# Forty of block 0's weighted rows on the tensor engine in a decoder layer

## The chip, the cores and the metric

The kernel runs on one core of one Trainium2 chip. Time is device time in microseconds, from the first to the last instruction of the program. The program's instructions are put in order once, before it runs: a scheduler lays out a queue for each engine (PE for matrix products, DVE for vectors, ACT for scalar functions and copies, POOL, which here issues the gathers, and SP, which issues the other loads and stores), and each engine works through its queue in that order, waiting on semaphores.

## The reference

One decoder layer over 512 tokens of width 1024, all in float32. The input projection feeds two groups of heads, and their outputs go through one output projection, a residual and a layer norm. Then comes a feed-forward part in which each token picks 128 of 16,384 single-neuron experts:

```python
proj = x @ w_in
att_out = dsa_attention(q_att, rms_norm(c_kv), q_idx, k_idx, w_idx, w_uk, w_uv)  # 128 best causal keys a query
hg_out = hgrn2(hg_q, hg_f, hg_i, hg_gate, lower_bound, g_norm)                   # gated recurrence, chunks of 32
mix = concatenate([att_out, hg_out]) @ w_out
h = layer_norm(ALPHA * x + mix)
# feed-forward, per token t: 8 heads x 16 experts
s = einsum('thpd,hpkd->thpk', h @ w_q, sub_keys)      # two sets of 128 scores a head
experts, g = top 16 of the sums of the two top-16 sets, softmax over them
a = gelu(einsum('td,thkd->thk', h, u[experts]))
ffn = einsum('thk,thkd->td', g * a, v[experts])
y = layer_norm(ALPHA * h + ffn)
```

## The kernel before

The 512 tokens are four blocks of 128. A first stage takes block 0 through attention, recurrence, output projection, layer norm and the choice of its experts. A second stage does that for blocks 1, 2 and 3 together. Last comes the dense part: for blocks 2 and 3 all 16,384 experts are computed as matrix products, with the weights of the chosen ones and zeros elsewhere.

Blocks 0 and 1 get their experts as rows instead. For rank k a gather (L639, an indirect DMA that POOL issues) brings the k-th expert's row of u, or later of v, of all 128 tokens into a tile of 128x1024, 512 KB. A row of u is multiplied with the block's `hs` and summed on DVE (L663), which gives one column of `hd`; through gelu and the routing weights these columns become `gate`. A row of v is added to `hs`, weighted with its column of `gate` (L676, DVE). Of block 0's 128 rows of v the last 52 go to PE: ACT makes a diagonal matrix `dg` out of a column of `gate` (L692), two products of 128x512 add the row into two PSUM banks (L694, four passes of PE in the trace), and one DVE add for each bank brings the sum to `hs` (L699). 14 of them stand at the end of stage 2 (`pv`), 38 at the start of the dense part (`pw`); block 1's 256 rows run beside the dense part.

Block 0's rows are spread over stage 2 by hand: `pump(n)` takes the next n rows from the generator `peer_gather`, and the table PUMP says how many at each place (`"hgrn"` 1 at each of eight places and two at another, `"att"` 4 in each half of an attention block, `"mix"` 1, `"q0"` 7). Rows on DVE are pinned to the program's order; everything else the scheduler places where its own timing puts it.

A gather needs a free tile. There are four of its own (GB), and the tiles `hs1`, `hs2`, `hs3`, `hx0`, `hx1` that the kernel doesn't need yet are lent to it (`lent`), nine in turn. `mix_norm` takes `hs1` to `hs3` back for blocks 1 to 3 and loads x into them (L479).

The order of stage 2 in the program: projections, the choice of keys (`select`), the recurrence `hgrn` of blocks 1, 2 and 3, the projection `qa` of the attention's queries, `attention` of the three blocks, `mix_norm`, `queries`. In `attention` PE makes qlp (L429) from `qa`, then the scores `sp` (L439), DVE turns them into P with the row's extreme (L441), ACT takes the exponential, PE transposes (L451) and multiplies (L457, L463), and DVE writes the result into `mixT` (L470). Half a block's four heads are one turn of this. `mix_norm` multiplies `mixT` with the output weights (L491), DVE adds (L494) and does the layer norm (L131 to L144); `queries` transposes the result (hT, L213), projects it (pq, L523), makes scores (L527) and picks the top 16 with MAX8 and its kin (L537 on).

Of the kernel before, what the change touches and what calls it, by code (L numbers as in the profile page):

```python
# [9 lines left out]
F32 = mybir.dt.float32  # L10
# [5 lines left out]
ALU = mybir.AluOpType  # L16
# [9 lines left out]

HGB = 5
GB = 4
UB = 4
VB = 3  # L30
HLB = 6
# [4 lines left out]
PUMP = {"cw": 4, "qi": 4, "hf": 4, "hq": 4, "hi": 4, "hg": 3, "qa": 2, "hgrn": 1, "att": 4, "mix": 1, "sel": 2,  # L36
        "q0": 7, "q1": 0, "q2": 0, "q3": 0}

PEK1 = 14
PEK2 = 38  # L40
PEPRE = 8
# [10 lines left out]
def tile_decoder_layer(ctx, tc, a, out):  # L52
# [218 lines left out]
    def hgrn(b, pr, mixT):  # L271
# [7 lines left out]
        nc.scalar.activation(kk, f, AF.Copy, scale=-1.0, bias=1.0)  # L279
        if b:  # L280
            pump(PUMP["hgrn"])
        cp = bank(f"cum{b}", "hg")
        nc.tensor.matmul(cp, tri, lf, start=True, stop=True)
        rp = bank(f"rev{b}", "hg")
# [6 lines left out]
        nc.vector.tensor_tensor(qs, qs, e, op=ALU.mult)  # L291
        if b:
            pump(PUMP["hgrn"])
        kt = k2(f"kt{b}")
        nc.scalar.activation(kt, cp, AF.Exp, scale=-1.0)
        nc.vector.tensor_tensor(kt, kk, kt, op=ALU.mult)
# [4 lines left out]
        nc.scalar.activation(dec.rearrange("p a b -> p (a b)"), dp[:, :16], AF.Exp)  # L301
        if b:
            pump(PUMP["hgrn"])
        qT = transpose4(qs, f"hqT{b}", nc.scalar, tag="hg")
        kT = transpose4(kt, f"hkT{b}", nc.scalar, tag="hg")
        AT = [k2(f"AT{b}_{par}").rearrange("p (j t) -> p j t", j=4) for par in range(2)]
# [9 lines left out]
        for n in range(4):  # L316
            S.append(state[0])
            if b:
                pump(PUMP["hgrn"])
            dsp = bank(f"ds{b}_{n}", "hg")  # L320
            for h in range(8):
                nc.tensor.matmul(dsp[(h % 2) * 64:(h % 2) * 64 + 64, (h // 2) * 64:(h // 2) * 64 + 64],
                                 kk[n * 32:n * 32 + 32, h * 64:h * 64 + 64],
                                 v[n * 32:n * 32 + 32, h * 64:h * 64 + 64], start=True, stop=True)
            s_new = pre.tile([128, 4, 64], F32, name=f"S{b}_{n}", tag="hg_S", bufs=5)
            ds3 = dsp[:, :256].rearrange("p (j e) -> p j e", j=4)
            nc.vector.tensor_tensor(s_new, state[0], dec[:, :, n:n + 1].to_broadcast([128, 4, 64]), op=ALU.mult)
            nc.vector.tensor_tensor(s_new, s_new, ds3, op=ALU.add)
            state[0] = s_new
        if b:  # L330
            pump(PUMP["hgrn"])
        ot = k2(f"o{b}")
        o = ot.rearrange("p (j a e) -> p j a e", j=4, a=2)
        gs4 = gs.rearrange("p (j a e) -> p j a e", j=4, a=2)
# [322 lines left out]
    def peer_gather(b):  # L657

        hd = cst.tile([128, 128], F32, name=f"hd{b}", tag="hd")
        for k in range(128):  # L660
            g = gather(a["u"], b, k, "u")
            tc.keep_in_program_order(
                nc.vector.scalar_tensor_tensor(g, g, 1.0, hs[b], op0=ALU.mult, op1=ALU.mult,  # L663
                                               accum_out=hd[:, k:k + 1]))
            if k % 32 == 31:
                sl = slice(k - 31, k + 1)
                nc.scalar.activation(hd[:, sl], hd[:, sl], AF.Gelu_apprx_tanh)
                nc.vector.tensor_tensor(gate[:, b, sl], gate[:, b, sl], hd[:, sl], op=ALU.mult)
            rows[0] -= 1
            yield True  # L670
        weighted.add(b)
        tc.keep_in_program_order(nc.scalar.mul(hs[b], hs[b], ALPHA))
        for k in range(128 - (PEK1 + PEK2 if b == 0 else 0)):
            g = gather(a["v"], b, k, "v")
            tc.keep_in_program_order(
                nc.vector.scalar_tensor_tensor(hs[b], g, gate[:, b, k:k + 1], hs[b], op0=ALU.mult, op1=ALU.add))  # L676
            rows[0] -= 1
            yield True
        spent.add(b)

    weighted = set()
    spent = set()

    def pe_gather(n, p):

        while 0 not in weighted:
            pump(1)
        ks = [pe_left.pop(0) for _ in range(n)]
        for k in ks:
            g = gather(a["v"], 0, k, "v")  # L690
            dg = gat.tile([128, 128], F32, name=f"dg{k}", tag="dg", bufs=1)
            nc.scalar.mul(dg, ident, gate[:, 0, k:k + 1])  # L692
            for i in range(2):
                nc.tensor.matmul(p[i], dg, g[:, i * 512:(i + 1) * 512], start=(k == ks[0]), stop=(k == ks[-1]))  # L694
            if k != ks[-1]:
                yield
        for i in range(2):
            y = hs[0][:, i * 512:(i + 1) * 512]
            nc.vector.tensor_tensor(y, y, p[i], op=ALU.add)  # L699
        yield  # L700

    todo = []
    rows = [512 - PEK1 - PEK2]

    def pump(n):
        while n > 0 and todo:
            try:
                if not next(todo[0]):
                    return
                n -= 1  # L710
            except StopIteration:
                todo.pop(0)

    def dense(den, dps):
# [88 lines left out]
                    nc.tensor.matmul(acc[i][n], wt[:, sl], vt, start=(j == 0 and q == 0), stop=(j == 127 and q == 2))  # L803

        def residual():
            ia = gat.tile([128, 128], F32, name="ia", tag="dg", bufs=1)
            nc.scalar.mul(ia, ident, ALPHA)
            for i in range(nb):
                for n in range(2):
# [34 lines left out]
    def stage(blocks, xT):  # L844
# [12 lines left out]
        else:  # L857
# [3 lines left out]
            kv_norm(blocks, pr)  # L861
            pens = {b: select(b, pr[b]) for b in blocks}
            hp = hgrn_proj(blocks, xT)
        for i, b in enumerate(blocks):
            hgrn(b, hp[b], mixT[:, 4:8, i * 128:(i + 1) * 128])
        if blocks != [0]:
            feat_proj(blocks, xT, pr, "qa")
        for i, b in enumerate(blocks):
            attention(b, pr[b], pens[b], mixT[:, 0:4, i * 128:(i + 1) * 128])
        mix_norm(blocks, mixT)  # L870
# [72 lines left out]
```

## Time and profile before

| | us |
|---|---|
| median of 3 runs | 1611.0 (1610.07 to 1612.66) |
| the profiled execution | 1606.46 |
| its span | 1604.6 |
| DVE busy in it | 1383.7 |
| PE busy in it | 1446.5 |
| rows of v on DVE, blocks 0 and 1 (L676) | 261.4 |
| rows of u on DVE, blocks 0 and 1 (L663) | 307.2 |

L676 counts 204 instructions, 76 of block 0 and 128 of block 1; L663 and each of the two gather lines count 256. The profile names a waiting time by what ended it: "<-DVE gu L663" is an engine that stood until DVE had finished a row of u, "<-issue" is time in which an engine waited for nothing that the profile shows. A mean granted clock of 1.00 for PE is the 2.4 GHz level, 0.50 the 1.2 GHz level. Where a name stands without its number, as P or gv, the profile has left it out.

### The profile page before, as it was taken

The page shows a single profiled execution, that of the slowest core. Times are in us where ns is not written, and L with a number is a line of the kernel's source. Part 1 is how long each engine was busy: PE and PEld are TensorE (multiplying, and loading weights), DVE is VectorE, ACT ScalarE, POOL GpSimd, SP SyncE. Part 2 cuts the span into 40 slices and gives each one's busy share as a digit, 9 for nine tenths or more (in the row PEclk, how much of TensorE's full clock was granted, in tenths as well). Part 3 has the DMA queues.
Part 4 walks back from the last instruction along what each step waited for, and adds up shares of the span by engine and source line. Part 5 has one row for each costly group of instructions (what it writes and reads, how often), then busy time and mean ns, then how long its engine had stood idle before and what let it go on. Part 6 is the DMA issues. An engine that isn't in the chain of part 4 may idle for free. (4 is left out here: it accounts for less than half of the span.)

```text
span 1604.6 us, 24491 instructions
## 1 busy us (share of the span) xinstructions
PE 1446.5 (90%) x7858; PEld 1087.4 (68%) x7858; DVE 1383.7 (86%) x3263; ACT 708.0 (44%) x1501; POOL 673.9 (42%) x531
## 2 busy tenths in 40 slices
PE   8889899854788899789989999999999999999996
PEld 4568444543444565246668888888898889889995
DVE  4139999799966899998877989999998899999998
ACT  3302331122432122169984555555555555555553
POOL 0004633777744420355433444444443345534440
PEclk9999999855799899899999999999999999999998
DMA  8378987899967770467668999999999999999995
GB/s 291 125 277 301 348 268 232 290 344 330 351 242 255 263 285 11 145 203 222 218 235 301 350 340 337 353 349 352 352 357 326 336 349 362 351 352 350 355 367 189
DMA packets 166161, 467.89 MB, mean 292 GB/s; under 512 B 18576, under 2 KB 18704, under 8 KB 165904
## 3 DMA queue, kind: packets, MB, share of 16 engines
q0 software_dynamic: 73728, 268.47, 48.0%
q1 hardware_dynamic: 92304, 197.86, 34.3%
q8 instruction: 62, 1.02, 0.2%
q14 instruction: 67, 0.55, 0.1%
HBM read 464.16 MB, written 2.10 MB: 291 GB/s over the span
## 5 line engine op out<-in xcount | busy, mean ns | idle before, releaser
L639 POOL DMA_INDIRECT gv<-in_v_dram,idx x256 | 333.1, 1301 | 417.4 <-DVE hs L676 263.3
L639 POOL DMA_INDIRECT gu<-in_u_dram,idx x256 | 330.9, 1293 | 409.8 <-DVE gu L663 259.1
L663 DVE SCALAR_TENSOR_TENSOR gu<-gu,hs 128x1024 f32<-128x1024 f32 x256 | 307.2, 1222 | 28.0 <-DMA gu<-in_u_dram,idx 27.8
L676 DVE SCALAR_TENSOR_TENSOR hs<-gv,gate,hs 128x1024 f32<-128x1024 f32 x204 | 261.4, 1281 | 9.7 <-DMA gv<-in_v_dram,idx 7.8
L772 ACT CAST v_0h<-v 128x512 fp32r<-128x512 f32 x128 | 79.7, 623 | 95.7 <-PE acc L803 60.9
L523 PE MATMUL pq<-hT,wpq 128*128 128x128 f32 (+1 forms) x512 | 121.3, 396 | 0.0
L774 DVE TENSOR_TENSOR u_0l<-u,u_0h 128x512 fp32r<-128x512 f32 x128 | 88.5, 691 | 35.6 <-ACT u_0h L772 32.6
L772 ACT CAST v_1h<-v 128x512 fp32r<-128x512 f32 x128 | 79.5, 621 | 87.7 <-DMA v<-in_v_dram 42.8
L772 ACT CAST u_0h<-u 128x512 fp32r<-128x512 f32 x128 | 79.4, 620 | 78.0 <-PE hp L783 41.1
L803 PE MATMUL acc<-v_0h,wl 128*128 128x512 f32 x256 | 102.0, 399 | 4.9 <-DVE wl L793 4.9
L523 PEld LDWEIGHTS pq<-hT,wpq 128*128 128x128 f32 x512 | 81.2, 201 | 33.4 <-issue 3.9
L803 PE MATMUL acc<-v_0h,wh 128*128 128x512 f32 x256 | 101.0, 395 | 0.0
L772 ACT CAST u_1h<-u 128x512 fp32r<-128x512 f32 x128 | 79.4, 621 | 48.2 <-PE acc L803 44.6
L774 DVE TENSOR_TENSOR v_1l<-v,v_1h 128x512 fp32r<-128x512 f32 x128 | 87.8, 686 | 14.3 <-ACT v_1h L772 13.5
L803 PE MATMUL acc<-v_1h,wh 128*128 128x512 f32 x256 | 99.7, 389 | 0.0
L803 PE MATMUL acc<-v_1h,wl 128*128 128x512 f32 x256 | 99.7, 389 | 0.0
L803 PE MATMUL acc<-v_0l,wh 128*128 128x512 f32 x256 | 99.5, 390 | 0.0
L774 DVE TENSOR_TENSOR u_1l<-u,u_1h 128x512 fp32r<-128x512 f32 x128 | 87.7, 685 | 4.5 <-ACT wh L791 3.5
L783 PE MATMUL hp<-hTl,u_0h 128*128 128x256 f32 x512 | 84.3, 287 | 8.0 <-ACT u_0h L772 8.0
L783 PEld LDWEIGHTS hp<-hTl,u_0h 128*128 128x128 f32 x512 | 76.7, 189 | 20.8 <-ACT u_0h L772 12.4
L774 DVE TENSOR_TENSOR v_0l<-v,v_0h 128x512 fp32r<-128x512 f32 x128 | 88.1, 688 | 2.5 <-ACT v_0h L772 1.6
L783 PE MATMUL hp<-hTh,u_1l 128*128 128x256 f32 x512 | 83.9, 286 | 5.1 <-DVE u_1l L774 5.1
(277 smaller groups left out, 3137.9 us busy)
## 6 DMA issues: line engine op xcount, KB each, us to landing
v<-in_v_dram SPq DMA_DIRECT2D x256, 256.0 KB, 6.2
u<-in_ut_dram SPq DMA_DIRECT2D x256, 256.0 KB, 6.0
wpq<-in_w_pq_dram SPq DMA_DIRECT2D x32, 512.0 KB, 4.7
wo<-in_w_o_dram SPq DMA_DIRECT2D x16, 512.0 KB, 7.6
hfw<-in_w_hf_dram SPq DMA_DIRECT2D x8, 512.0 KB, 6.8
hqw<-in_w_hq_dram SPq DMA_DIRECT2D x8, 512.0 KB, 9.1
hiw<-in_w_hi_dram SPq DMA_DIRECT2D x8, 512.0 KB, 4.9
qaw<-in_w_qa_dram SPq DMA_DIRECT2D x8, 512.0 KB, 5.1
```

What stands on the lines that cost most here:

```text
L523: nc.tensor.matmul(qp[:, :nt], w[:, k, :], hT[:, k, :nt], start=(k == 0), stop=(k == 7))
L639: nc.gpsimd.indirect_dma_start(out=t, out_offset=None, in_=table, in_offset=bass.IndirectOffsetOnAxis(ap=idx[b][k // 64][:, k % 64:k % 64 ...
L663: nc.vector.scalar_tensor_tensor(g, g, 1.0, hs[b], op0=ALU.mult, op1=ALU.mult, accum_out=hd[:, k:k + 1]))
L676: nc.vector.scalar_tensor_tensor(hs[b], g, gate[:, b, k:k + 1], hs[b], op0=ALU.mult, op1=ALU.add))
L772: nc.scalar.copy(h, x)
L774: nc.vector.tensor_tensor(l, x, h.bitcast(F32), op=ALU.subtract)
L783: nc.tensor.matmul(hp, ut[:, k * 128:(k + 1) * 128], ht[n][:, k, :], start=(n + q + k == 0), stop=(n == 1 and q == 2 and k == 3))
L803: nc.tensor.matmul(acc[i][n], wt[:, sl], vt, start=(j == 0 and q == 0), stop=(j == 127 and q == 2))
```

## The change

The first 40 rows of v of block 0 (PEK0) go to PE as well, in a new generator `pe_head`. It takes the tile `hx1` out of the lent ones and makes it an accumulator `vacc`, so eight tiles are left for gathers. Each row is gathered, gets its `dg` from ACT and is added by two products into two banks `ph`, the first of the two pinned to the program's order. After each eighth row the banks are brought to `vacc`: the first time by two ACT copies, then four times by two DVE adds of 128x512. At the end one DVE add of 128x1024 brings `vacc` to `hs0`. `pump_pe` asks for one row at each of eight places in hgrn 1 and for two at each in hgrn 2 and 3; what is left is asked for behind hgrn 3, where the order of the program now has no `qa` any more, since its projection is called ahead of hgrn. DVE keeps 36 rows of v of block 0 (40 to 75). There are two buffers for `dg` where there was one. The total that the dense part spreads over its loop (`rows`) takes off the 40.

```diff
+DGB = 2
+PEK0 = 40
@@ hgrn: at eight places
         if b:
             pump(PUMP["hgrn"])
+            pump_pe(min(b, 2))
@@ peer_gather
-        for k in range(128 - (PEK1 + PEK2 if b == 0 else 0)):
+        for k in range(PEK0, 128 - PEK1 - PEK2) if b == 0 else range(128):
@@ new
+    def pe_head():
+        lent.remove("hx1")
+        vacc = cst.tile([128, 1024], F32, name="vacc", tag="hx1")
+        for k in range(PEK0):
+            if k % 8 == 0:
+                p = [bank(f"ph{k}_{i}") for i in range(2)]
+            g = gather(a["v"], 0, k, "v")
+            dg = gat.tile([128, 128], F32, name=f"dg{k}", tag="dg", bufs=DGB)
+            nc.scalar.mul(dg, ident, gate[:, 0, k:k + 1])
+            for i in range(2):
+                mm = nc.tensor.matmul(p[i], dg, g[:, i * 512:(i + 1) * 512], start=(k % 8 == 0), stop=(k % 8 == 7))
+                if i == 0:
+                    tc.keep_in_program_order(mm)
+            if k % 8 == 7:
+                for i in range(2):
+                    y = vacc[:, i * 512:(i + 1) * 512]
+                    if k == 7:
+                        nc.scalar.copy(y, p[i])
+                    else:
+                        nc.vector.tensor_tensor(y, y, p[i], op=ALU.add)
+            yield
+        while 0 not in weighted:
+            pump(1)
+        nc.vector.tensor_tensor(hs[0], hs[0], vacc, op=ALU.add)
+        yield
+    def pump_pe(n):
+        if not head:
+            head.append(pe_head())
+        for _ in range(n):
+            next(head[0], None)
@@ pe_gather (and the same for ia in residual)
-            dg = gat.tile([128, 128], F32, name=f"dg{k}", tag="dg", bufs=1)
+            dg = gat.tile([128, 128], F32, name=f"dg{k}", tag="dg", bufs=DGB)
@@
-    rows = [512 - PEK1 - PEK2]
+    rows = [512 - PEK0 - PEK1 - PEK2]
@@ stage
+        if blocks != [0]:
+            feat_proj(blocks, xT, pr, "qa")
         for i, b in enumerate(blocks):
             hgrn(b, hp[b], mixT[:, 4:8, i * 128:(i + 1) * 128])
         if blocks != [0]:
-            feat_proj(blocks, xT, pr, "qa")
+            pump_pe(PEK0 + 1)
```

On PE, in the kernel before, the first scores of block 1's attention (sp1_0 to sp1_2) stand between the last products of hgrn 1 (o1_1, hoT1) and the first of hgrn 2 (cum2):

```order
L344 MATMUL o1_1_2186<-S1_0_2106,hqT1_2071 32x64
L344 MATMUL o1_1_2186<-S1_1_2121,hqT1_2071 32x64
L344 MATMUL o1_1_2186<-S1_2_2136,hqT1_2071 32x64
L439 MATMUL sp1_0_2752<-ckvT_102,qlT1_2736 128x256
L439 MATMUL sp1_1_2757<-ckvT_102,qlT1_2736 128x256
L439 MATMUL sp1_2_2762<-ckvT_102,qlT1_2736 128x256
L213 MATMUL hoT1_ps_2233<-ident_61,o1_2157 128x128 x4
```

In the changed kernel the scores of block 1 stand among the last of the 40 rows (ph32, the banks of rows 32 to 39):

```order
L699 MATMUL ph32_0_2818<-gv0_37_2880,dg37_2882 128x512
L699 MATMUL ph32_1_2819<-gv0_37_2880,dg37_2882 128x512
L446 MATMUL sp1_0_3014<-ckvT_102,qlT1_2998 128x256
L699 MATMUL ph32_0_2818<-gv0_38_2901,dg38_2903 128x512
L699 MATMUL ph32_1_2819<-gv0_38_2901,dg38_2903 128x512
L699 MATMUL ph32_0_2818<-gv0_39_2907,dg39_2909 128x512
L699 MATMUL ph32_1_2819<-gv0_39_2907,dg39_2909 128x512
L446 MATMUL sp1_1_3019<-ckvT_102,qlT1_2998 128x256
L446 MATMUL sp1_2_3024<-ckvT_102,qlT1_2998 128x256
```

hgrn 2 and 3 and rows 0 to 37 stand ahead of sp1_0 now, and two more rows ahead of sp1_1.

On DVE, in the kernel before, the first P of block 1 stand behind a row of u, gu0_125, and the first multiplication of hgrn 3's output (S3 and o3 are of hgrn 3):

```order
L663 SCALAR_TENSOR_TENSOR gu0_123_2333,hd0_1170<-gu0_123_2333,hs0_104 128x1024
L328 TENSOR_TENSOR S3_3_2572<-S3_3_2572,ds3_3_2563 128x256
L663 SCALAR_TENSOR_TENSOR gu0_124_2348,hd0_1170<-gu0_124_2348,hs0_104 128x1024
L663 SCALAR_TENSOR_TENSOR gu0_125_2363,hd0_1170<-gu0_125_2363,hs0_104 128x1024
L351 TENSOR_TENSOR o3_2578<-o3_0_2581,gs3_2027 128x4x64
L441 ISA P1_0_2754,nmx1_2749<-sp1_0_2752,isc1_1380 128x256
L441 ISA nmx1_2749 128x1
L441 ISA P1_1_2759,nmx1_2749<-sp1_1_2757,isc1_1380 128x256
```

In the changed kernel rows of v and the adds into vacc stand ahead of them:

```order
L683 SCALAR_TENSOR_TENSOR hs0_104<-gv0_53_2844,gate_114,hs0_104 128x1024
L683 SCALAR_TENSOR_TENSOR hs0_104<-gv0_54_2871,gate_114,hs0_104 128x1024
L683 SCALAR_TENSOR_TENSOR hs0_104<-gv0_55_2898,gate_114,hs0_104 128x1024
L448 ISA P1_0_3016,nmx1_3011<-sp1_0_3014,isc1_1380 128x256
L448 ISA nmx1_3011 128x1
L683 SCALAR_TENSOR_TENSOR hs0_104<-gv0_56_2970,gate_114,hs0_104 128x1024
L708 TENSOR_TENSOR vacc_2116<-vacc_2116,ph32_0_2818 128x512
L683 SCALAR_TENSOR_TENSOR hs0_104<-gv0_57_2973,gate_114,hs0_104 128x1024
L708 TENSOR_TENSOR vacc_2116<-vacc_2116,ph32_1_2819 128x512
L448 ISA P1_1_3021,nmx1_3011<-sp1_1_3019,isc1_1380 128x256
```

All rows of u, rows 40 to 55 of v and the adds of ph8 to ph24 stand ahead of P1_0 now, rows 56 and 57 and the adds of ph32 ahead of P1_1. On POOL the first 108 gathers are the same in both kernels; behind them the rows of v of the two engines are interleaved with the last 20 rows of u, gv0_55 is the 182nd gather, gv0_39 the 183rd and gv0_57 the 186th.

## Rows read from the trace of the kernel before

**Rows 1.** Page: busy time by engine; groups: busy and mean ns | idle before.

```profile
PE 1446.5 (90%) x7858; PEld 1087.4 (68%) x7858; DVE 1383.7 (86%) x3263; ACT 708.0 (44%) x1501; POOL 673.9 (42%) x531
...
L676 DVE SCALAR_TENSOR_TENSOR hs<-gv,gate,hs 128x1024 f32<-128x1024 f32 x204 | 261.4, 1281 | 9.7 <-DMA gv<-in_v_dram,idx 7.8
```

**Rows 2.** Busy time by stretches: length, engines (instructions), PE clock, DMA, GB/s.

```profile
284.12:465.02 180.90, 119.50 (x686) 72.98 (x684) 165.82 (x311) 49.99 (x135) 142.65 (x116) 0.69 0.92 333
320.00:340.00 20.00, 10.31 (x42) 6.52 (x39) 19.43 (x46) 8.27 (x19) 14.61 (x12) 0.59 0.99 385
320.00:416.00 96.00, 51.09 (x394) 35.72 (x391) 93.20 (x199) 28.00 (x79) 74.50 (x61) 0.52 0.94 346
365.00:374.00 9.00, 0.00 (x0) 0.00 (x0) 9.00 (x21) 0.00 (x0) 6.87 (x8) 0.50 0.97 352
405.20:434.90 29.70, 20.02 (x86) 10.97 (x86) 28.54 (x55) 14.45 (x38) 23.72 (x21) 0.73 0.97 357
434.90:467.70 32.80, 27.27 (x101) 13.50 (x100) 27.07 (x36) 10.76 (x27) 24.60 (x22) 0.95 0.92 334
437.15:454.54 17.39, 14.74 (x50) 6.90 (x49) 17.07 (x23) 4.88 (x14) 13.73 (x12) 1.00 0.91 326
467.70:502.30 34.60, 29.19 (x105) 13.62 (x103) 18.95 (x32) 13.39 (x29) 6.38 (x6) 1.00 0.45 148
540.00:582.00 42.00, 42.00 (x141) 25.73 (x140) 34.25 (x50) 6.01 (x13) 27.88 (x24) 0.95 0.97 370
640.00:668.00 28.00, 23.02 (x59) 9.22 (x58) 28.00 (x186) 6.06 (x14) 11.25 (x10) 1.00 0.58 169
```

**Rows 3.** DVE timeline: start, length, line, operation [idle before <- releaser].

```profile
405.24 0.41 DVE L441 CUSTOM_DVE_ANT_0 P<-sp,isc 128x256 f32<-128x256 f32 x1
...
405.58 0.41 DVE L441 CUSTOM_DVE_ANT_0 P<-sp,isc 128x256 f32<-128x256 f32 x1
...
501.58 0.69 DVE L470 TENSOR_TENSOR mixT<-oT,rT 128x512 f32<-128x512 f32 x1 [1.33 <-ACT rT L108]
...
575.85 0.48 DVE L537 MAX8 sv<-pss 128x8 f32<-128x128 f32 x2
```

**Rows 4.** POOL timeline, three gathers.

```profile
367.10 0.94 POOL L639 DMA_INDIRECT gu<-in_u_dram,idx  x1 [0.30 <-issue]
...
400.51 1.17 POOL L639 DMA_INDIRECT gv<-in_v_dram,idx  x1 [0.30 <-issue]
...
464.05 0.94 POOL L639 DMA_INDIRECT gv<-in_v_dram,idx  x1 [0.30 <-issue]
```

**Rows 5.** Groups by line, POOL, 284 to 465 us.

```profile
L639 POOL DMA_INDIRECT gu<-in_u_dram,idx x71 | 91.1, 1284 | 28.3 <-issue 16.5 <-DVE gu L663 6.1 <-DVE rs_thg L118 1.5
L639 POOL DMA_INDIRECT gv<-in_v_dram,idx x43 | 50.5, 1175 | 13.3 <-issue 10.5 <-DVE nmx L441 1.8 <-DVE rs_thg L119 0.6
```

**Rows 6.** Groups by line, PE, 640 to 668 us.

```profile
L694 PE MATMUL pv<-gv,dg 128*128 128x512 f32 x43 | 21.2, 614 | 5.0 <-ACT dg L692 5.0
```

**Rows 7.** PE timeline, first row after a wait.

```profile
674.89 3.78 PE L694 MATMUL pv<-gv,dg 128*128 128x512 f32 x4 [6.28 <-ACT dg L692]
```

**Rows 8.** DMA issues, 284 to 465 us: count, median us to landing.

```profile
gu<-in_u_dram,idx POOLq DMA_INDIRECT x71, 6.3
gv<-in_v_dram,idx POOLq DMA_INDIRECT x43, 6.2
```

**Rows 9.** Groups by line, DVE, 405.2 to 502.3 and 502.3 to 575.8 us.

```profile
L676 DVE SCALAR_TENSOR_TENSOR hs<-gv,gate,hs 128x1024 f32<-128x1024 f32 x43 | 55.4, 1288 | 0.8
...
L676 DVE SCALAR_TENSOR_TENSOR hs<-gv,gate,hs 128x1024 f32<-128x1024 f32 x32 | 41.1, 1284 | 7.8 <-DMA gv<-in_v_dram,idx 7.0
```

**Rows 10.** PE timeline, mix and two transposes of hT.

```profile
502.33 27.73 PE L491 MATMUL mix<-wo,mixT 128*128 128x512 f32 x64 [1.46 <-DVE mixT L470]
...
533.67 1.56 PE L213 MATMUL hT_ps<-ident,hs 128*128 128x128 f32 x8 [1.62 <-DVE vel L134]
538.34 1.94 PE L213 MATMUL hT_ps<-ident,hs 128*128 128x128 f32 x8 [3.11 <-DVE hs L144]
```

More of the change, by code (lines that the diff above doesn't have):

```diff
@@ L293, in hgrn @@
             pump(PUMP["hgrn"])
+            pump_pe(min(b, 2))
         kt = k2(f"kt{b}")
@@ L303, in hgrn @@
             pump(PUMP["hgrn"])
+            pump_pe(min(b, 2))
         qT = transpose4(qs, f"hqT{b}", nc.scalar, tag="hg")
@@ L319, in hgrn @@
                 pump(PUMP["hgrn"])
+                pump_pe(min(b, 2))
             dsp = bank(f"ds{b}_{n}", "hg")
@@ L331, in hgrn @@
             pump(PUMP["hgrn"])
+            pump_pe(min(b, 2))
         ot = k2(f"o{b}")
@@ L679, in peer_gather @@
         spent.add(b)
+    def pe_head():
[23 more added lines that the diff above has]
+        yield
+    head = []
+    def pump_pe(n):
[3 more added lines that the diff above has]
+            next(head[0], None)
     weighted = set()
@@ L805, in residual @@
         def residual():
-            ia = gat.tile([128, 128], F32, name="ia", tag="dg", bufs=1)
+            ia = gat.tile([128, 128], F32, name="ia", tag="dg", bufs=DGB)
             nc.scalar.mul(ia, ident, ALPHA)
```

## The prediction

> **What bounds the kernel now.** I read the page first, then the busy time by stretches, then the timelines of DVE and POOL over 367 to 576 us, then the groups by line inside the same stretches. On the page DVE and PE both look full [rows 1], which says nothing yet about the part that changes. By stretches it is clearer [rows 2]: from 284 to 465 us DVE is busy 165.8 of 180.9 us while the DMA engines stand at 0.92 and PE at a mean granted clock of 0.69; from 540 to 582 us PE has no idle time at all (42.00 of 42.00). The 40 rows that leave DVE come out of a stretch where DVE and the gathers are both close to full.
>
> What releases the next piece of the layer is read from the DVE timeline [rows 3]. The first P of block 1 runs at 405.24 us, the second at 405.58, the last mixT (block 3) at 501.58, the first top-k instruction at 575.85. Behind that one come the routing and the dense part, in which the change touches nothing but the number of dg buffers; so the end of the program moves by what the first top-k instruction moves.
>
> Next the gathers, which POOL issues one by one. gv_0 is the 129th, issued at 400.51; the 171st is issued at 464.05, and counted back from gv_0 the one at 367.10 is the 108th, gu_107 [rows 4]. Through here POOL waits for almost nothing that another engine does: before the 114 gathers of 284 to 465 us 27.0 us of its idle time are "issue" (16.5 + 10.5) and 6.1 a wait for a tile that DVE's rows free [rows 5]. So the gathers set their own pace. It is 1.59 us each from 367.10 to 400.51 (21 intervals), 1.51 from 400.51 to 464.05 (42), 1.45 inside 437.15 to 454.54 (12 in 17.39 us [rows 2]), and 1.24 at the quickest, as at 367.10 (0.94 and the 0.30 ahead of it).
>
> **The change part by part.** *Work that leaves DVE.* 40 of L676 at 1.281 us [rows 1] are 51.2 us less. Added on DVE are 8 adds of 128x512 out of PSUM, for which mixT, 128x512 out of PSUM as well, has a row of 0.69 us [rows 3], and one add of 128x1024, about one L676: 5.5 + 1.3 = 6.8 us. Net 44.4 us less. That is the gain, and it counts only where DVE is what the next stage waits for.
>
> *Where the 40 rows now stand.* In the kernel before, the P instructions of block 1 stand in DVE's queue right after gu_125, and their sp in PE's queue ahead of hgrn 2. In the changed one the first P stands behind gv_55 and the second behind gv_57 and the adds of ph32; on PE sp1_1 stands behind the matmuls of gv_39. Each engine runs its queue in order, so block 1's attention can't get going before those gathers have landed. In POOL's queue all gathers up to the 108th are the same in both kernels; gv_55 is the 182nd now, gv_39 the 183rd, gv_57 the 186th, where 126 were needed ahead of the first P.
>
> *Its price.* From 367.10 on, hgrn 3 lies beside the next 21 gathers as before, at 1.59 us, to 400.5; the 54 from there to the 183rd are plain rows, for which I take the 1.45 of the stretch that holds only such rows and attention: 78.3 us, an issue at 478.8. A gather lands 6.3 us after its issue (gu; gv 6.2 [rows 8]); then the row's four passes on PE, of which 43 take 21.2 us at full clock, are 1.98 us [rows 6]. 478.8 + 6.3 + 2.0 = 487.1, so the second P runs at about 487.4 in place of 405.58: **+82 us**. The ends: all 75 gathers from 367.10 on at 1.24 are 93.0 us, P at 468.7 (+63); all at 1.59 are 119.3, P at 495.0 (+89). The diag matrix on ACT costs nothing here: PE waits 5.0 us for 43 passes' worth of it with one buffer [rows 6], and now there are two, beside gathers that come slower than PE's rows.
>
> The Trainium skill, "DMA: Bandwidth & Descriptors", section "Where 436 GB/s comes from", holds that a transfer between HBM and SBUF is bound on HBM's side at about 358 GB/s; the 524,288 bytes of a gather would then need 1.46 us, an estimate, none could run closer than that, and P would come at +80 at least. The trace disagrees, with 385 GB/s over 320 to 340 us [rows 2], so 1.24 stays the lower end.
>
> *What is won back in attention.* From the second P to the last mixT it takes 96.0 us now. DVE runs 43 rows of L676 in it [rows 9]; after the change 18 stand behind the second P, and one add of 128x1024. Blocks 1 and 2, where DVE is busy 28.5 of 29.7 and 27.1 of 32.8 us [rows 2], become looser; block 3, with 18.95 of 34.6, is bound by its own chain already. PE's work over the three is 20.0 + 27.3 + 29.2 = 76.5 us, so less than about 75 is not to be had; the other end is no gain. I take 85, the middle: **-11 us** (0 to -21).
>
> *What is won back in mix and the queries.* 32 rows of L676, 41.1 us of DVE, stand between 502.3 and 575.8 us, with 7.0 us of waiting for gv [rows 9]; after the change none. But the stretch is PE's: mix takes 27.73 us in one piece, two transposes of hT are held up 1.62 and 3.11 us by the layer norm on DVE [rows 10], and then pq runs without a gap. The holds, 4.7 us, are what the rows' absence can give back: **-5 us** (-3 to -8).
>
> *Small edits.* With two dg buffers the rows of pv can lose PE's 5.0 us of waiting for dg, but DVE is full there (28.00 of 28.00 us in 640 to 668 [rows 2]): -1 us (0 to -1.5). The loads of hs for blocks 1 to 3 wait for tiles that the gathers borrow, and those are given back at another time: between nothing and one landing of 6.3 us (512 KB as well): +2 us (0 to +6). qa's projection ahead of hgrn moves PE work into a stretch where PE is half idle (51.1 of 96.0 us busy in 320 to 416 [rows 2]): 0. One tile fewer for gathers (8 for 9): a tile's turn of 0.94 + 6.3 + 1.28 = 8.5 us over 8 tiles allows one gather per 1.07 us, below the 1.24: 0.
>
> **Sum.** +82 - 11 - 5 - 1 + 2 = +67 us on a span of 1604.6 us. The profiled execution took 1606.46 us and the median of the runs is 1611.0, 4.5 us above it; the sum is set on the median: **1678 us**. Ends: 63 - 21 - 8 - 1.5 + 0 = +32 (1643) and 89 - 0 - 3 - 0 + 6 = +92 (1703).
>
> **Rivals.** *The gathers catch up.* PE takes two rows of three, tiles come free sooner, gathers go at 1.24 throughout, and a lean DVE lets attention run at PE's 75 us: +32 to +45, some 1649 us. For it: in 365 to 374 us POOL did issue 8 in 9.00 us, with the DMA engines at 0.97 [rows 2]. Against it: POOL waits for tiles only 6.1 us now, so that free tiles can hardly hasten it.
>
> Another cause of slow gathers would be DVE. The Trainium skill, "SBUF — State Buffer", section "SBUF: two separate sides", says that while DVE runs in a mode that takes both ports, GpSimd can't write the descriptors of its DMAs; if rows of L663 and L676 did that, fewer of them on DVE would free the gathers and this rival would hold. The trace speaks against it: the quick gathers of 365 to 374 us fall where DVE has no idle time at all, 9.00 of 9.00 us [rows 2].
>
> *PE is the new bound.* Where PE comes out of a wait its clock is 0.50 (the 1.2 GHz level) and a row takes 3.78 us [rows 7]; in 320 to 416 us the mean granted clock is 0.52 [rows 2]. If the 34 rows from gv_6 on ran so from about 403 us, they would end at 403 + 34 x 3.78 = 531, P at +126, and with the same gains the time were some 1720 us. Against it: with rows close behind one another the clock stood at 1.00 in 640 to 668 us.
>
> *DVE sets the end after all* (the other side): if the P instructions were not held by the order, 44.4 us less DVE work between 367 and 502 us would make the layer faster, 1611 - 44 = 1567 us. It needs 186 gathers by about 405 us, where the program has made 131 by then, and decides only if the second P comes before about 420 us (what attention and queries win back is 16). Nothing speaks for it but DVE's row on the page.
>
> **How the numbers follow.** Forecast 0.62, gathers catch up 0.19, PE the new bound 0.12, DVE the end 0.04, delay and gains cancel 0.03. The range is the sum's two ends, 1643 to 1703; it leaves out the PE case, the faster one and the one that cancels. A difference below 0.2% (about 3 us) can't be told from none here. Faster 0.04, the same 0.02, slower 0.94.
>
> **What would show it.** In the profile after: the second P of block 1 near 487 us (460 to 470 would mean that the gathers caught up, over 510 a slow PE, under 420 that I misread the queues); gathers from 400 to 479 us at 1.4 to 1.5 us each with POOL waiting for "issue"; DVE with idle time ahead of P that ends with gv or with PE's ph; PE's rows at 1.98 us; from the first top-k instruction on the same picture as now, some 67 us later. What would make it wrong above all: gathers that wait for tiles held by either of two consumers, PE or DVE, which the trace of before can't show.

## The result, and the profile after

| | before | changed |
|---|---|---|
| median of 4 runs, us | 1611.83 (1610.07 to 1617.54) | 1691.76 (1684.93 to 1696.68) |
| ratio | | 1.0478 (95%: 1.0435 to 1.0521) |
| span of the profiled execution, us | 1604.6 | 1686.7 |

The change makes the kernel 80 us slower. The prediction was 1678 us, 1643 to 1703, so it held; the delay is 13 us longer than the sum. By the page of the changed kernel, DVE has lost 42 us of work (1383.7 to 1341.6 [rows 1]) and PE has gained 60:

```profile
PE 1506.2 (89%) x8018; PEld 1114.8 (66%) x8018; DVE 1341.6 (80%) x3232; ACT 724.9 (43%) x1543; POOL 660.4 (39%) x531
...
L683 DVE SCALAR_TENSOR_TENSOR hs<-gv,gate,hs 128x1024 f32<-128x1024 f32 x164 | 209.8, 1279 | 33.9 <-DMA gv<-in_v_dram,idx 32.9
```

Where the time went is read from a few instructions of the DVE timeline, those of [rows 3], here in the changed kernel (the first two P of block 1, mixT of block 3, the first top-k):

```profile
494.12 0.42 DVE L448 CUSTOM_DVE_ANT_0 P<-sp,isc 128x256 f32<-128x256 f32 x1 [2.70 <-PE sp L446]
...
499.09 0.42 DVE L448 CUSTOM_DVE_ANT_0 P<-sp,isc 128x256 f32<-128x256 f32 x1
...
583.36 0.69 DVE L477 TENSOR_TENSOR mixT<-oT,rT 128x512 f32<-128x512 f32 x1 [9.79 <-ACT rT L110]
...
652.52 0.87 DVE L544 MAX8 sv<-pss 128x8 f32<-128x128 f32 x4 [28.23 <-ACT pss L539]
```

| us | before | changed | shift | length of the stretch: change |
|---|---|---|---|---|
| second P of block 1 | 405.6 | 499.1 | +93.5 | +93.5 |
| last mixT | 501.6 | 583.4 | +81.8 | -11.7 |
| first top-k | 575.9 | 652.5 | +76.7 | -5.1 |
| last idx (rows below) | 701.7 | 774.6 | +72.9 | -3.8 |
| first product of the dense loop, acc | 851.1 | 932.6 | +81.5 | +8.6 |
| end of the span | 1604.6 | 1686.7 | +82.1 | +0.6 |

93.5 us are lost ahead of P; attention, mix and queries win back 16.8 and the routing 3.8 (no run here shows why the routing did); between the last idx and the dense loop 8.6 us are lost that the prediction did not have.

The 5.1 us of mix and queries do not come from PE's waiting for the layer norm. By groups of PE from the last mixT to the first top-k, the transposes of hT wait as long as before; here before, then changed:

```profile
L213 PE MATMUL hT_ps<-ident,hs 128*128 128x128 f32 x24 | 4.6, 353 | 5.6 <-DVE hs L144 4.0 <-DVE vel L134 1.6
```

```profile
L215 PE MATMUL hT_ps<-ident,hs 128*128 128x128 f32 x24 | 3.9, 326 | 5.3 <-DVE hs L146 5.3
```

What changed is DVE's queue. Before, ACT's copy of the first scores (pss) starts at 572.5, and the top-k stands behind three rows of v until 575.85; in the changed kernel the copy starts at 651.9 and the top-k, for which DVE sits idle, follows 0.6 us later. That is 2.8 of the 5.1 us; the copy itself comes 2.4 us earlier behind the last mixT.

Ahead of P, the POOL timeline shows the 108th gather, the 129th and the 183rd (gv_39); before, the first two were at 367.10 and 400.51 [rows 4]:

```profile
368.93 1.18 POOL L646 DMA_INDIRECT gu<-in_u_dram,idx  x1 [0.30 <-issue]
...
404.58 0.94 POOL L646 DMA_INDIRECT gv<-in_v_dram,idx  x1 [4.68 <-PE ph L699]
...
485.41 0.93 POOL L646 DMA_INDIRECT gv<-in_v_dram,idx  x1 [0.30 <-issue]
```

The 75 gathers take 116.5 us, 1.55 each. By groups, POOL over these 75 now waits for PE's rows too, 11.9 us, which [rows 5] has not at all:

```profile
L646 POOL DMA_INDIRECT gv<-in_v_dram,idx x54 | 58.1, 1076 | 27.6 <-PE ph L699 11.9 <-issue 11.0 <-DVE hs L683 3.2
L646 POOL DMA_INDIRECT gu<-in_u_dram,idx x21 | 24.4, 1163 | 6.4 <-issue 4.9 <-DVE gu L670 0.3 <-DVE f L276 0.3
```

By stretches (columns as in [rows 2]): 410 to 485.4 us, up to gv_39's issue, and 453.7 to 494 within it, where no hgrn is left; then attention, mix and queries up to the first top-k, the routing, and the dense part's head:

```profile
410.00:485.40 75.40, 63.53 (x199) 27.63 (x199) 30.86 (x46) 18.43 (x55) 53.14 (x51) 0.95 0.96 349
453.70:494.00 40.30, 32.87 (x86) 14.28 (x85) 16.44 (x15) 7.87 (x19) 31.43 (x30) 1.00 1.00 379
...
499.10:583.40 84.30, 72.14 (x274) 35.66 (x274) 40.53 (x76) 32.68 (x77) 22.48 (x20) 0.96 0.40 138
583.40:652.50 69.10, 63.12 (x200) 35.30 (x201) 20.91 (x58) 7.91 (x16) 0.00 (x0) 0.95 0.35 115
652.50:774.60 122.10, 109.92 (x342) 58.97 (x341) 118.15 (x795) 33.20 (x65) 24.26 (x24) 0.96 0.39 127
774.60:932.60 158.00, 126.23 (x684) 91.82 (x683) 125.06 (x239) 136.55 (x329) 57.02 (x53) 0.93 0.61 195
```

From 410 to 485 us DVE is busy 30.9 of 75.4 us: it is not the bound any more. The DMA engines stand at 0.96 and PE is busy for 63.5. In the groups of DVE over 404 to 499 us its rows wait 32.9 us for gv, in those of PE over 404 to 496 the new rows wait 10.1:

```profile
L683 DVE SCALAR_TENSOR_TENSOR hs<-gv,gate,hs 128x1024 f32<-128x1024 f32 x18 | 23.1, 1283 | 33.2 <-DMA gv<-in_v_dram,idx 32.9 <-ACT hs L679 0.3
```

```profile
L699 PE MATMUL ph<-gv,dg 128*128 128x512 f32 x154 | 73.8, 624 | 11.9 <-DMA gv<-in_v_dram,idx 10.1 <-DVE vacc L708 1.8
```

And this is the end of the 40 rows on PE. gv_39, issued at 485.41, ends with the passes of 493.91 to 497.51, 12.1 us after its issue, because PE still has the rows ahead of it to do; sp of the second P comes right behind:

```profile
485.23 3.70 PE L699 MATMUL ph<-gv,dg 128*128 128x512 f32 x8
...
489.94 3.70 PE L699 MATMUL ph<-gv,dg 128*128 128x512 f32 x8
493.48 0.59 PE L446 MATMUL sp<-ckvT,qlT 128*128 128x256 f32 x2
493.91 3.60 PE L699 MATMUL ph<-gv,dg 128*128 128x512 f32 x8
497.35 1.03 PE L446 MATMUL sp<-ckvT,qlT 128*128 128x256 f32 x4
```

### The profile page after: what moved, and what is told of

Its sections match the earlier page's. It is cut to its first block, busy times and chain, and to the rows that moved or that the text cites. A ratio compares the mean times of both kernels' runs of the same rounds, so it can differ in the third digit from the quotient of the medians.

```text
span 1686.7 us, 24843 instructions
## 1 busy us (share of the span) xinstructions
PE 1506.2 (89%) x8018; PEld 1114.8 (66%) x8018; DVE 1341.6 (80%) x3232; ACT 724.9 (43%) x1543; POOL 660.4 (39%) x531
## 5 line engine op out<-in xcount | busy, mean ns | idle before, releaser
L646 POOL DMA_INDIRECT gv<-in_v_dram,idx x256 | 324.9, 1269 | 491.3 <-DVE hs L683 244.9
L646 POOL DMA_INDIRECT gu<-in_u_dram,idx x256 | 325.5, 1271 | 422.8 <-DVE gu L670 243.5
L670 DVE SCALAR_TENSOR_TENSOR gu<-gu,hs 128x1024 f32<-128x1024 f32 x256 | 307.3, 1221 | 15.6 <-DMA gu<-in_u_dram,idx 15.4
L683 DVE SCALAR_TENSOR_TENSOR hs<-gv,gate,hs 128x1024 f32<-128x1024 f32 x164 | 209.8, 1279 | 33.9 <-DMA gv<-in_v_dram,idx 32.9
L736 PE MATMUL pw<-gv,dg 128*128 128x512 f32 x152 | 79.7, 656 | 31.3 <-DMA gv<-in_v_dram,idx 22.9
L789 DVE TENSOR_TENSOR og<-iota,dtr 128x512 f32<-128x512 f32 x128 | 81.4, 686 | 25.7 <-PE gb L798 22.6
```

Of the source, the lines that this page charges most:

```text
L646: nc.gpsimd.indirect_dma_start(out=t, out_offset=None, in_=table, in_offset=bass.IndirectOffsetOnAxis(ap=idx[b][k // 64][:, k % 64:k % 64 ...
L789: nc.vector.tensor_tensor(og[n], iota[:, None, :].to_broadcast([128, 4, 128]), x[n][:, c:c + 4, None].to_broadcast([128, 4, 128]), op=ALU. ...
```

## The experiments

Eleven kernels, in three groups (x1 to x4, x5 to x8, x9 to x11), each on one chip, where the kernel before took 1628.1, 1630.4 and 1617.8 us. So ratios to the kernel before on the same chip are compared (the changed kernel: 1.0478); single instants of these profiles lie up to 4% later than on the first chip (P at 420.0 in x6, where the same 126 rows stand ahead of it as at 405.6 in the kernel before). P stands for the second P of block 1.

**Gathers or PE.** *x1: the 40 rows without their gathers.*

```diff
-            g = gather(a["v"], 0, k, "v")
+            g = consts_loaded["wuv"].rearrange("p a b -> p (a b)")
...
-                mm = nc.tensor.matmul(p[i], dg, g[:, i * 512:(i + 1) * 512], ...)
+                mm = nc.tensor.matmul(p[i], dg, g, ...)
```

> The changed kernel, but the 40 rows on the tensor engine multiply a constant tile that lies in SBUF already: their 40 gathers are left out, everything else of them (diag, two products each, adds) stays. The computation is not the layer's. Theory 'the gathers set when attention begins': gv_57 is now the 146th gather in place of the 186th; 38 gathers after the 108th (368.9) at 1.45 us end at about 424, so the second P of block 1 comes near 435 (499.1 in the changed kernel) and the time falls by some 50 to 60 us, to about 1635. Rival 'the tensor engine is as much the bound': 34 rows behind hgrn 3 at 1.85 us from about 405 to 425 on end at 470 to 488, so the second P comes at 470 to 490 and the time falls by only 5 to 25 us, to 1670 to 1685.

Measured: ratio 1.0291 (1.0225 to 1.0358), 1.9% of 1628 us, 30 us, less than the changed kernel. P, and PE in the stretch ahead of it:

```profile
471.61 0.42 DVE L448 CUSTOM_DVE_ANT_0 P<-sp,isc 128x256 f32<-128x256 f32 x1
```

```profile
403.00:471.00 68.00, 68.00 (x324) 34.11 (x323) 41.83 (x68) 23.93 (x62) 31.37 (x26) 1.00 0.65 215
```

P comes at 471.6, in the rival's range: with no gather of these rows to wait for, PE is busy for 68.00 of 68.00 us at the 2.4 GHz level, and holds P until about 470 by itself. The time lies between the two ranges (1.0291 of 1611.8 is 1659).

*x2: all gathers, half the products.*

```diff
             for i in range(2):
+                if i == 0 or k % 8 == 7:
-                mm = nc.tensor.matmul(...)
+                    mm = nc.tensor.matmul(...)
```

> The changed kernel with one product of 128x512 for each of the 40 rows in place of two (the second half only for each eighth row): all gathers stay, the tensor engine has about 35 x 0.93 = 32 us less. The computation is not the layer's. Theory 'gathers': the issue of gv_39 (485.4) moves by little, and only the backlog on the tensor engine behind the last landing goes (491 to 497.5): second P at about 490 to 494, time 5 to 10 us less, about 1683. Rival 'tensor engine': the second P comes 25 to 32 us earlier, at about 470, time about 1662.

Measured: ratio 1.0443 (1.038 to 1.0505), not told apart from the changed kernel. P at 505.5; the 183rd gather at 490.96, 75 gathers in 115.2 us. P, POOL's groups over these gathers, and the stretch of 409 to 505 us (columns as in [rows 2]):

```profile
505.52 0.42 DVE L448 CUSTOM_DVE_ANT_0 P<-sp,isc 128x256 f32<-128x256 f32 x1
```

```profile
L646 POOL DMA_INDIRECT gv<-in_v_dram,idx x54 | 58.9, 1091 | 24.0 <-issue 13.1 <-PE ph L700 8.7 <-PE o L351 1.1
L646 POOL DMA_INDIRECT gu<-in_u_dram,idx x21 | 23.3, 1109 | 9.0 <-issue 4.6 <-PE ph L700 1.8 <-DVE rs_thg L117 1.7
```

```profile
409.00:505.00 96.00, 68.36 (x218) 26.00 (x218) 42.09 (x63) 22.99 (x65) 69.33 (x63) 0.81 0.93 338
```

Half the products less bring nothing: the gathers by themselves hold P as long. (PE's busy time fell by less than the 32 us reckoned, to 68.4 of 96.0 us from 82.5 of 95.0 over 404 to 499 in the changed kernel, since its mean granted clock there was 0.81 for 0.96; but it was idle for 27.6 us and so did not bind.) That is the theory's side; its own figure of 490 to 494 us was for the first chip, and in this order P stands behind gv_57 and the last add besides.

*x9: neither the gathers nor the second products.* Both diffs together.

> The changed kernel with both taken away: the 40 rows multiply a constant tile (no gathers of theirs) and make one product in place of two. The computation is not the layer's. Without the gathers alone the second P came at 471.6, with half the products alone at 505.5 (499.1 in the changed kernel, 405.6 in the one before). Theory 'gathers and tensor engine are two bounds that lie 28 us apart': with both gone only hgrn 3 and the 146 gathers that are left hold P, which comes at 435 to 450, and the time is 1.0 to 2.0% above the kernel before, of which 0.7% is the second dg buffer. Rival 'a third thing (pinning, PSUM ring) holds P': 465 or later, 2.5% or more.

Measured: ratio 1.0112 (1.0064 to 1.016), P at 435.6:

```profile
435.64 0.42 DVE L448 CUSTOM_DVE_ANT_0 P<-sp,isc 128x256 f32<-128x256 f32 x1
```

So it is as the theory had it: two bounds side by side, PE's up to about 471 (x1) and the gathers' up to about 505 (x2), and either of them hides part of what the other's removal would bring. Of the 4.8%, 3.7 go when both are gone. What holds P at 435.6 is neither: from 419.4 us, when `gate` is done, to 435.3 DVE runs its own rows of v and adds without a gap, 15.9 of 15.9 us, beside a PE busy for 15.8.

**How many rows.** *x8: 16 rows in place of 40.*

```diff
-PEK0 = 40
+PEK0 = 16
```

> The changed kernel with 16 rows on the tensor engine in place of 40; nothing is left out. In the queues the second P stands behind gv_15, the 147th gather (183rd with 40 rows). Theory 'gathers ahead of P, 1.55 us each': gv_15 is issued at about 368.9 + 39 x 1.55 = 429, the second P comes at about 440 (499 with 40 rows, 405.6 with none); after what attention and queries win back (17 us with 40 rows, 8 to 17 here) the time is 1.0 to 1.7% above the kernel before. Rival 'a fixed cost of the new rows (PSUM ring, pinning, qa, lent tile)': second P at 470 or later and over 3%.

Measured: ratio 1.0143 (1.0071 to 1.0214), in the theory's range; P at 451.2, 11 us later than it said, which had counted from the first chip's 405.6:

```profile
451.23 0.42 DVE L448 CUSTOM_DVE_ANT_0 P<-sp,isc 128x256 f32<-128x256 f32 x1
```

16 rows cost 1.4% and 40 cost 4.8%. Beside x6's P of 420.0 on the same chip, the 21 gathers more ahead of P (147 for 126) moved it by 31 us, 1.5 each, for 34 forecast. Between 16 rows and 40 lie 36 gathers ahead of P (147 and 183); at 1.55 us each they are 56 us, and the times differ by 3.4%, some 55 us.

**Another place.** *x3: the 40 rows behind attention.*

```diff
-            pump_pe(min(b, 2))      (at the eight places in hgrn)
-            pump_pe(PEK0 + 1)       (ahead of attention)
+            pump_pe(PEK0 + 1)       (behind attention, ahead of mix_norm)
```

> The changed kernel, but the 40 rows are asked for behind the attention of block 3 and ahead of the output projection, and none in hgrn; nothing is left out. Block 1's attention is no longer behind them. Theory 'the delay is work on gathers and tensor engine that has to lie somewhere': the second P of block 1 comes at 405 to 412 as in the kernel before, and the 74 us of products go in among attention and output projection, where the tensor engine is busy 76.5 of 97 us and then without a gap; time 1611 + 74 - 20 to 30 of idle time filled = 1655 to 1665. Rival 'only the place ahead of attention costs': time within 10 us of the kernel before, 1611 to 1620.

Measured: ratio 1.042 (1.0371 to 1.0469). P at 421.3, the first top-k at 648.1. By groups of PE from 512 us on, behind the last mixT:

```profile
L699 PE MATMUL ph<-gv,dg 128*128 128x512 f32 x160 | 69.6, 593 | 0.0
L498 PE MATMUL mix<-wo,mixT 128*128 128x512 f32 x64 | 28.2, 594 | 1.6 <-DVE hs L501 1.6
L215 PE MATMUL hT_ps<-ident,hs 128*128 128x128 f32 x24 | 3.2, 276 | 4.2 <-DVE hs L146 3.0 <-DVE vacc L708 1.2
```

P is early again, and the time all but the same: 160 passes, the whole 40 rows, take 69.6 us of PE behind the last mixT and have no idle time ahead of any of them, where PE was full already. So the rival falls, and the theory's cost was too low (1.042 of 1611.8 is about 1680): I had expected 20 to 30 us of PE's gaps in attention to be filled, and none were, and the dg buffer's share was not in it.

*x4: the sums in hgrn's PSUM ring.*

```diff
-                p = [bank(f"ph{k}_{i}") for i in range(2)]
+                p = [bank(f"ph{k}_{i}", "hg") for i in range(2)]
```

> The changed kernel with the two sums of eight rows in the PSUM ring of hgrn (five banks) in place of the ring of three that attention uses; nothing is left out. In the tensor engine's queue the first scores of block 1 stand ahead of hgrn 2 again; on the vector engine the first P still stands behind gv_55 (181st gather) and the adds of the fourth group. Theory 'order on the vector engine': the second P comes at about 490 (gv_55 issued at about 483, landed at 489), time 5 to 10 us less than the changed kernel, about 1683. Rival 'the ring of three PSUM banks holds attention back': the second P near 410 to 430 and a time of 1615 to 1630.

Measured: ratio 1.0622 (1.057 to 1.0673), slower than the changed kernel; both theories missed. P at 521.9. The PE timeline at the ends of hgrn 1 and hgrn 2 (columns as in [rows 7]), and what stands right ahead of the first P (521.60) on DVE:

```profile
428.77 1.08 PE L215 MATMUL hoT_ps<-ident,o 128*128 128x128 f32 x4 [8.42 <-DVE o L365]
429.65 4.89 PE L699 MATMUL ph<-gv,dg 128*128 128x512 f32 x8
...
480.94 1.09 PE L215 MATMUL hoT_ps<-ident,o 128*128 128x128 f32 x4 [8.15 <-DVE o L365]
481.82 6.11 PE L699 MATMUL ph<-gv,dg 128*128 128x512 f32 x8
```

```profile
521.26 0.42 DVE L358 TENSOR_TENSOR o<-o,gs 128x256 f32<-128x256 f32 x1 [6.77 <-ACT sq L356]
```

At the end of hgrn 1 and of hgrn 2 PE stands 8 us for DVE's o with the next row behind it in the queue, and from the one to the other it takes 52 us; the rows are strung through the three blocks' hgrn, one behind the other. That the ring shared with hgrn forced this order is likely, but only argued. With sp early in PE's queue again P came no earlier: it stands in DVE's queue behind the first multiplication of hgrn 3's output, which waited 6.77 us for ACT, and not for a row of v, the last of which was done by 514.5. So it is order on DVE that held P, but through a late hgrn 3.

**The second dg buffer.** *x5: the changed kernel with one buffer. x6: the kernel before with two.*

```diff
-DGB = 2
+DGB = 1                                              (x5)
-            dg = gat.tile(..., tag="dg", bufs=1)
+            dg = gat.tile(..., tag="dg", bufs=2)     (x6, and the same for ia)
```

> The changed kernel with one dg buffer, as before; nothing is left out. From the first og to the first acc, the dense part's head takes 148.5 us in the kernel before (702.55 to 851.1) and 154.6 in the changed one (778.0 to 932.6), with the tensor engine waiting 22.9 us for gv. Theory 'the second dg buffer lets the scheduler put pw products ahead of their gathers': 148 to 150 us here, time 4.4% above the kernel before in place of 4.8%. Rival 'the two buffers have nothing to do with it': 154 to 155 us.

> The kernel before with two dg buffers and no other change. Theory 'second dg buffer costs in the dense part': head of the dense part 153 to 156 us in place of 148.5, and 0.2 to 0.4% slower. Rival 'no effect, or the 1 us that I gave it': 147 to 149 us and within 0.2%.

Measured: x5 1.0456 (1.0383 to 1.0529), which the interval can't tell from 1.0478; x6 1.0072 (1.0039 to 1.0106), slower, 11 to 12 us. The stretch from the last idx to the first acc is read from the source lines (first and last start of each group); here x5, then x6:

```profile
L627 DVE SCALAR_TENSOR_TENSOR idx<-dc_v,dc_v x4: 205/217/224, 138.0 to 795.1; 128x64 uint32<-128x64 f32 x4
...
L845 PE MATMUL acc<-v_0h,wl x256: 387/395/497, 943.3 to 1681.8; 128*128 128x512 f32 x128
```

```profile
L620 DVE SCALAR_TENSOR_TENSOR idx<-dc_v,dc_v x4: 194/218/224, 141.4 to 726.6; 128x64 uint32<-128x64 f32 x4
...
L803 PE MATMUL acc<-v_0h,wl x256: 387/395/628, 896.0 to 1641.4; 128*128 128x512 f32 x128
```

With one buffer it is 149.4 (before), 148.2 (x5) and 149.7 us (x7, below), with two 158.0 (changed), 169.4 (x6) and 157.5 to 165.0 (x1 to x4, x8, x9); x10 and x11 below, with one buffer but more rows left for the queries, take 156.7 each, so other things lengthen it too. (The profiled execution of x6 took 1657.7 us for a median of 1642.3, so its 169.4 may be above what it mostly takes.) (The expectations count it from the first og, which gives 148.5 and 154.6 for the kernels before and changed.) By groups, all of PE's pw rows in x6:

```profile
L694 PE MATMUL pw<-gv,dg 128*128 128x512 f32 x152 | 78.6, 648 | 41.0 <-DMA gv<-in_v_dram,idx 33.1 <-ACT tab L610 7.7
```

and POOL's gathers at the head of it, 690 to 760 us:

```profile
L639 POOL DMA_INDIRECT gv<-in_v_dram,idx x13 | 23.4, 1804 | 26.7 <-PE pw L694 21.0 <-PE pv L694 3.3 <-issue 1.2
L639 POOL DMA_INDIRECT gu<-in_u_dram,idx x5 | 5.4, 1084 | 15.0 <-PE pw L694 14.7 <-issue 0.3
```

In the kernel before pw waits 9.9 us in all, for dg, and nothing for gv. With a second buffer its rows follow one another closely at the head of the queue, 16 of their products ahead of the first transposition of the dense part (dtp) where 4 stood; gathers have only their own four tiles there, so that PE waits for gv and POOL for a tile from PE in turn, and dtp and gb, for which the G loop waits, stand behind. In the changed kernel 18 products stand ahead of dtp and pw waits 22.9 us for gv; in x5, with one buffer, 6 do, and pw waits 9.1 us for dg and 2.1 for gv. That the second buffer makes the kernel before slower is shown by x6's time; the chain of tile, gather and queue is read from the waits and was not tried by itself.

That x5's time came out no better than the changed kernel's has a likely reason in its trace: the second buffer is worth something ahead of P. By groups of PE over 404 to 508 us, the 40 rows in x5:

```profile
L699 PE MATMUL ph<-gv,dg 128*128 128x512 f32 x144 | 73.1, 630 | 18.6 <-ACT dg L697 13.0 <-DMA gv<-in_v_dram,idx 2.8 <-DVE vacc L708 1.4
```

With one buffer they wait 13.0 us for dg, with two (the group of 404 to 496 us above) not at all. P comes at 508.7 in x5, on another chip than the 499.1. So in the changed kernel the second buffer seems to win ahead of P about what it loses ahead of the dense loop; 0.7% is its price in the kernel before, and can't be taken off the changed kernel's 4.8%.

**qa.** *x7: only qa's projection ahead of hgrn.*

```diff
+        if blocks != [0]:
+            feat_proj(blocks, xT, pr, "qa")
         for i, b in enumerate(blocks):
             hgrn(...)
-        if blocks != [0]:
-            feat_proj(blocks, xT, pr, "qa")
```

> The kernel before with qa's projection called ahead of hgrn and no other change. On the vector engine the first P now stands behind gu_127 and three rows of v where it stood behind gu_125. Prediction's value for it: 0, second P within 4 us of 405.6. Rival, from the kernel with the rows asked for late (second P 421.3 us): the projection's place alone costs 8 to 16 us at P, and 0.2 to 0.7% of the time.

Measured: ratio 0.9984 (0.9953 to 1.0016), no difference. P at 427.8, outside the 4 us expected; beside 420.0 in x6 on the same chip it is 8 us late, as the rival had it, but they are given back: the first top-k is at 598.3 beside 603.3. The prediction's 0 holds for the time.

**Fewer rows ahead of attention.** *x10 and x11: the kernel before with another PUMP table.*

```diff
-"hi": 4, "hg": 3, "hgrn": 1, "att": 4, "mix": 1
+"hi": 4, "hg": 3, "hgrn": 0, "att": 6, "mix": 3      (x10)
+"hi": 3, "hg": 2, "hgrn": 0, "att": 8, "mix": 3      (x11)
```

> The kernel before with none of block 0's rows asked for in hgrn (0 for 1 at each place), 6 for 4 in each half of an attention block and 3 for 1 at each place of the output projection: the same 204 rows, 18 fewer ahead of the first P (gu_107 for gu_125). Theory 'each gather ahead of P costs what it takes': second P 15 to 25 us earlier than with gu_125, and the time 0.5 to 1.0% below the kernel before, as long as the last rows don't hold the first top-k. Rival 'the time ahead of P is hgrn's chain and the rows fill its gaps': second P within 6 us, time the same or up to 1% slower because more rows stand behind the output projection.

> As the kernel with none of block 0's rows in hgrn, with 3 for 4 and 2 for 3 in the projections hi and hg as well, 8 in each half of attention and 3 at each place of the output projection: gu_99 stands ahead of the first P. Theory 'gathers ahead of P': a further 8 to 12 us earlier P, the time 0.7 to 1.5% below the kernel before. Rival 'rows must be done by the top-k': the first top-k waits for rows behind it and the time is equal or above.

Measured: x10 1.0097 (1.0068 to 1.0127), x11 1.0114 (1.0063 to 1.0164): slower. P comes early, 393.5 and 389.6, and it brings nothing; nor is it as early as the theory said (12 us ahead of 405.6 for 15 to 25, then 4 more for 8 to 12). In both it follows right on the first multiplication of hgrn 3's output (392.8 and 388.9), which waited 2.3 us for ACT: there hgrn's chain is the limit, as the rival had it. x10, the first two P, the last row ahead of the first top-k, and that; then PE's transposes of hT:

```profile
393.12 0.41 DVE L441 CUSTOM_DVE_ANT_0 P<-sp,isc 128x256 f32<-128x256 f32 x1
...
393.45 0.42 DVE L441 CUSTOM_DVE_ANT_0 P<-sp,isc 128x256 f32<-128x256 f32 x1
...
595.25 1.28 DVE L676 SCALAR_TENSOR_TENSOR hs<-gv,gate,hs 128x1024 f32<-128x1024 f32 x1 [0.92 <-DMA gv<-in_v_dram,idx]
596.45 2.41 DVE L537 MAX8 sv<-pss 128x8 f32<-128x128 f32 x12
```

```profile
L213 PE MATMUL hT_ps<-ident,hs 128*128 128x128 f32 x24 | 5.6, 423 | 17.7 <-DVE hs L144 17.7
```

Rows that no longer stand ahead of P stand among the attention, the layer norm and the top-k. In x10 attention takes 113.1 us (96.0 before); behind the last mixT DVE has 48 rows of v for 32, and PE waits 17.7 us for the layer norm on DVE, where it waited 5.6; ACT's copy of the first scores starts at 591.4, and the rows hold the top-k until 596.5. Of the three tables tried the one of the kernel before is the best, and no kernel tried here is faster than it beyond its interval.

## Why the prediction was right, and which terms were off

- *The order decides* (P behind gv_39 and gv_57): right. P moved by +93.5 us for +82, 4 us beyond the upper end that I had given this step. gv_39 was issued at 485.4 for 478.8: 1.8 us because the 108th was later already, 4.8 because the 75 gathers took 116.5 us for 111.7. POOL waited 11.9 us for tiles that PE's rows held. I had named that (tiles held by either of two consumers) as what the trace of before can't show, and had given it no price: a tile's turn of 8.5 us counted no waiting in PE's queue. The other 5 us lie between gv_39's issue and P, 13.7 us for 8.6: 3.8 are PE's rows still ahead of its own, and 1.3 the row of v and the add that stand ahead of P on DVE (499.1 for an end of PE's passes at 497.5). That this step left its own range and the time did not leave the whole one is luck in part: the range adds up all ends at once, the upper with no gain in attention. The tile fewer (8 for 9, put at 0) was not tried by itself.
- *PE as the bound* was put down at 0.12 and only for the 1.2 GHz level. x1 shows that it binds at the 2.4 GHz level too, by its work alone. That the gathers outlast it by some 34 us (505.5 in x2 against 471.6 in x1, on one chip) is why the sum by gathers came out; had the gathers come at 1.24 us, PE would have held P near the lower end's 468.7 all the same, which the prediction had not reckoned.
- *Attention* (-11): 96.0 to 84.3 us, -11.7. As forecast, the first two blocks won and the third did not: up to their mixT the three take 18.8, 29.8 and 35.8 us for 28.6, 32.9 and 34.6. The size was the middle between PE's sum and no gain, so that it fits so well is luck. *Mix and queries* (-5): -5.1, the right number by the wrong cause. The holds that were to go, 4.7 us, are still there (5.3 us for 5.6 in all); the gain came from the top-k, which no longer stands behind rows of v, and from earlier scores.
- *Two dg buffers* (-1, 0 to -1.5): the step that failed as a mechanism. The stretch up to the dense loop took +8.6 us in the changed kernel, and the second buffer alone cost 0.72% in the kernel before (x6). I costed it by the wait that it removes, and not by what the freed rows then run into: four tiles, and the dense part's first products behind them in the queue. What I had put at nothing for the 40 rows, their waiting for dg, is nothing only because there are two (13.0 us with one, x5).
- *The loads of hs* (+2, 0 to +6) don't show: DVE waits for none of them in the changed kernel. *qa* (0): between -0.5 and +0.2% (x7).
- *The gathers catch up*: fell for the whole; 1.23 us came in single gathers (485.41 with the 0.30 ahead of it), 1.55 in the mean. In part it was there: without hgrn beside them, over 453.7 to 494 us, 30 gathers came at 1.38 us each. Waits for tiles, 15.4 us over the 75, took that back. So the mean that the sum took, 1.49, came near because two things that it left out work against each other. By an estimate from the rule of the Trainium skill, "DMA: Bandwidth & Descriptors", section "Where 436 GB/s comes from" (HBM's side at about 358 GB/s), P would have come at +80 at least, nearer to what came than my lower end; but the trace still disagrees with the figure, with 379 GB/s over 453.7 to 494 us.
- *DVE sets the end*: fell; the 42 us that it lost brought the gains in attention and at the top-k and nothing ahead of P, where DVE was idle for 44.5 of 75.4 us.

## What to carry to other kernels

Work moved to another engine takes its transfers and its place in two queues with it: count what stands ahead of the next stage's first instruction in each queue, transfers first, before the busy time that it frees. Where a transfer stream and an engine are nearly equal as bounds, taking either away alone tells little; take both. A deeper buffer that removes a wait should be costed, at each place that uses it, by what the freed instructions wait for next, and by who stands behind them.

## What was not expected of the hardware

The gathers went quicker beside an idle DVE, and the mean hides it. In the kernel before, 12 gathers of 437.15 to 454.54 us, beside a DVE busy for 17.07 of 17.39 us, took POOL 1.14 us each and came every 1.45 us, at a DMA share of 0.91 [rows 2]. In the changed kernel, 30 gathers of 453.7 to 494 us, beside a DVE busy for 16.44 of 40.30 us, took 1.05 us each and came every 1.38 us, at a DMA share of 1.00. Over all 75 the mean is 1.55 us as before (1.54 from the 108th to the 171st), because POOL now waits 15.4 us for tiles. The Trainium skill, "SBUF — State Buffer", section "SBUF: two separate sides", has DVE keep GpSimd from writing descriptors in its two-port modes. These rows would fit that, and the quick gathers beside a full DVE at 365 to 374 us [rows 2] do not; no run here changes DVE's load alone, nor parts POOL's issuing from the DMA engines as what sets the pace, so both stay open.
